# A two-layer hybrid DiT block: residual stores by unit from SP, squares in three tiles, weight loads at the start held back

## The chip, the cores and the metric

The kernel runs on one core of a Trainium2 chip. Its time is device microseconds of one execution, the median of several runs. The profile comes from one more execution. The engines are TensorE (PE, with its weight loads as PEld), VectorE (DVE), ScalarE (ACT), GpSimd (POOL) and SyncE (SP, which here only issues DMAs). Each engine works through its own queue strictly in order. A DMA is issued by an instruction in the queue of SP or POOL, which waits there until its data and its target are ready.

## The reference

Two layers of a transformer block on 512 tokens x (A) and 256 context tokens (C), with D = 1024 and a hidden width of 2816:

```python
for i in range(2):
    mx, mc = modulation(c, ada_w[i], ada_b[i]), modulation(c_ctx, ada_w[i], ada_b[i])
    x  = x  + 0.5*mx[2]*swiglu(pre_norm(x,  norm1_g[i], mx[0], mx[1]), ffn1...)
    xc = xc + 0.5*mc[2]*swiglu(pre_norm(xc, norm1_g[i], mc[0], mc[1]), ffn1...)
    ux, uc = pre_norm(x, norm2_g[i], mx[3], mx[4]) @ w_in[i], pre_norm(xc, ...) @ w_in[i]
    y, yc = four mixers (windowed attention, gated delta net, MLA, neighbourhood attention)
    x  = x  + mx[5] * (y @ w_out[i])
    x  = x  + 0.5*mx[8]*swiglu(pre_norm(x, norm3_g[i], mx[6], mx[7]), ffn2...)
    # the same for xc in layer 0 only
return rms_norm(x, final_norm_g)
# pre_norm(h, g, shift, scale) = rms_norm(h, g) * (1 + scale) + shift
# modulation(c, w, b) = silu(c) @ w + b, in nine parts
```

## The kernel before

The residual X lies in SBUF as `[128, 8, 768]`: eight chunks m (or k) of 128 features, 512 columns of A and 256 of C. A is cut into the units A0 and A1 of 256 columns; with C there are three units. Every product is made of three matmuls (`mm3`) of high and low halves, which is why each weight is loaded (`raw`, tile `wr`), cast on ACT (`wh`) and its rest formed on DVE (`wl`).

The stages are: start; first FFN of layer 0; mixers; `second_half` (output projection and second FFN); the same for layer 1. `ffn2` is the FFN of three of the four places (both layers' first FFN, and layer 0's second). It forms the hidden activations group by group and adds each group's down projection to X by an accumulating DMA from POOL (L509, from a tile `y`). For the last group it goes unit by unit, `PASSES[2]` = C, A0, A1, and for each unit through the eight chunks m (`down(..., True)`): 12 matmuls into `dacc`, then x is updated on DVE (L503), squared on ACT into a tile `sq` (L282) and the square added to the unit's sum `ss` on POOL (L283; on DVE for A1 from chunk 5). If the caller asks (`save`), chunk m of the unit is stored to DRAM from POOL's queue (L507, tensor `xd`); both first FFNs ask for it, for C and A in layer 0 and for A in layer 1, because `second_half` loads X back from there. Two chunks into the next unit (`LAG` = 2) `then(u)` is called for the unit before. It is `norm`: four `nsum` matmuls sum over partitions (L294), DVE and POOL form the reciprocal root (L308, L310), DVE a diagonal `dg` (L297), PE spreads it (`rb`, L301), and per chunk there are one ACT operation (L328) and two DVE operations (L324, L329) that write the next stage's input `xn`.

`sq` is one tile in these stages, shared by tag with an unused output of the adaLN reductions on DVE (`adao`, L211); in the last FFN (`ffn`) there are two.

The mixers start with projections `pj` from the weights `win` (loaded by SP, L350); the tiles of the mixers lie over X and the FFN's weight tiles, and wait for these tile by tile.

At the start SP loads X, then 32 tiles of adaLN weights `adaw` (L178, 256 KB each), which PE multiplies with silu(c) (L179). `ada_row` loads `silr` (L165, 1 MB, silu'd on ACT), which only the later adaLN reductions on DVE need. Then C, A0 and A1 are squared and normed, and the FFN's weights are asked for by `raw` in 256 KB loads, in eight tiles by turns.

The order in each engine's queue isn't the order of the code: a planner lays it down when the program is built, by simulating the engines and taking what it finds ready, earlier code first. So a stage's instructions may stand before or behind those of its neighbours.

Of the kernel before, what the change touches and what calls it, by code (L numbers as in the profile page):

```python
# [6 lines left out]
F32 = mybir.dt.float32  # L7
# [9 lines left out]
TX = 512  # L17
TC = 256
# [31 lines left out]
class Net:  # L50
# [111 lines left out]
    def ada_row(self):  # L162
        nc = self.nc
        self.silr = self.const.tile([128, 2, 1024], F32, name="silr")
        nc.sync.dma_start(out=self.silr, in_=self.I["crow"].rearrange("(o v) k -> o v k", o=1).to_broadcast([128, 2, 1024]))  # L165
        nc.scalar.activation(self.silr, self.silr, ACTF.Silu)

    def ada_first(self):

        nc = self.nc  # L170
        acc = self.psum(name="adaacc", ring="r")
        for k in range(KD):
            for g in range(4):
                if g >= 2:
                    w = self.wp.tile([128, 512], F32, tag="wr", name="adaw", bufs=RB)
                else:
                    w = self.hp.tile([128, 768], F32, tag=("hh", "hl")[g % 2], name="adaw")[:, :512]
                nc.sync.dma_start(out=w, in_=self.I["ada_w0"][k * 128:(k + 1) * 128, g * 512:(g + 1) * 512])  # L178
                nc.tensor.matmul(acc[32 * g:32 * g + 32, :], lhsT=self.silc[:, k], rhs=w,  # L179
                                 start=(k == 0), stop=(k == KD - 1), tile_position=(0, 32 * g))  # L180
        tp = self.ada_rows(acc)
        src = tp.rearrange("p s (g r) -> p g s r", r=32)[:, :, :, 0:2]
        self.ada_bias(0, 0, src, 4)
        self.mod_cols(0, 1, 2)
# [77 lines left out]
    def sumsq(self, u, m, eng=None):  # L262

        nc = self.nc
        p, c, t = self.unit(u)
        if self.wblk:
            if u == "A":
                for h in ("A0", "A1"):
                    self.sumsq(h, m, nc.vector)
                return  # L270
            if m == 0:
                self.ss[u] = self.wp.tile([128, 512], F32, tag="ws", name="ss" + u, bufs=4)[:, :t]
            ss = self.ss[u]
        else:
            if m == 0 and c.start == 0:
                self.ss[p] = self.fs.tile([128, self.T[p]], F32, tag="ss" + p, name="ss" + p, bufs=1)
            ss = self.ss[p][:, c]
        if m == 0:
            nc.scalar.activation(ss, self.X[p][:, m, c], ACTF.Square)
        else:  # L280
            sq = self.fs.tile([128, TX], F32, tag="sq", name="sq", bufs=1 if self.wblk else 2)[:, :t]
            nc.scalar.activation(sq, self.X[p][:, m, c], ACTF.Square)  # L282
            (eng or (nc.vector if u == "A" or (u in SSV and m >= SSM) else nc.gpsimd)).tensor_tensor(ss, ss, sq, op=ALU.add)  # L283

# [70 lines left out]

    def raw(self, ap):
        t = self.wp.tile([128, 512], F32, tag="wr", name="wr", bufs=RB)[:, :ap.shape[-1]]
        self.nc.sync.dma_start(out=t, in_=ap)
        return t

# [64 lines left out]
    def ffn2(self, l, i, save, then):  # L425
# [3 lines left out]
        nc = self.nc  # L429
# [48 lines left out]
        def down(f0, f1, m, us, last):  # L478
            nf = f1 - f0
            while (l, 3 * i + 2) not in self.adone:  # L480
                self.sided += 1
                next(self.side)
            ap = dn[l, fi, m, :, f0:f1].rearrange("p f c -> p (f c)")
            if not last:
                wh, wl = self.weight(ap, nf * 128)
            else:
                if m not in keep:
                    keep[m] = self.block(self.raw(ap), [keep[w][m // 3][:, m % 3] for w in "hl"])
                wh, wl = keep[m]
            for v in us:  # L490
                p, cols, t = self.unit(v)
                r = 0 if p == "A" else 1
                acc = self.psum((128, t), name="dacc", ring=None if last else "d")
                if not last and v == us[0]:
                    y = self.wp.tile([128, TX + TC], F32, tag="y", name="y", bufs=3)
                for f in range(f0, f1):
                    c = slice((f - f0) * 128, (f - f0) * 128 + 128)
                    self.mm3(self.two(acc, v), wh[:, c], wl[:, c], self.tok(H[f][0], v), self.tok(H[f][1], v), f == f0, f == f1 - 1)
                if not last:
                    nc.scalar.activation(y[:, 0:TX] if p == "A" else y[:, TX:], acc, ACTF.Copy, scale=gate[:, i, m, r:r + 1])  # L500
                    continue
                x = self.X[p][:, m, cols]
                nc.vector.scalar_tensor_tensor(out=x, in0=acc, scalar=gate[:, i, m, r:r + 1], in1=x,  # L503
                                               op0=ALU.mult, op1=ALU.add)
                self.sumsq(v, m)
                if p in save:
                    nc.gpsimd.dma_start(out=self.xd[p][:, m, cols], in_=x)  # L507
            if not last:
                nc.gpsimd.dma_start(out=self.X[""][:, m], in_=y, accum_op=ALU.add)  # L509

# [4 lines left out]
        for t, f, n in order:  # L515
            if n == 0:
                chunks[f] = self.chunk7(up[l, fi, f], hid, f)
            next(chunks[f], None)
            if n == SLOTS - 1 and f == GROUPS2[gi][1] - 1 and f < NF - 1:
                tasks += [(t + WAIT, *GROUPS2[gi], m) for m in range(KD)]  # L520
                gi += 1
            if tasks and tasks[0][0] <= t:
                down(*tasks.pop(0)[1:], ("C", "A"), False)
            fill(nc1, (t + 1) / SLOTS)
        for k in tasks:
            down(*k[1:], ("C", "A"), False)
        keep = {w: [self.tp7.tile([128, 3, 512], F32R, tag="t%s%d" % (w, n), name="wt" + w) for n in range(3)] for w in "hl"}
        due = []
        for us in PASSES[2]:
            for m in range(KD):  # L530
                if due and m >= LAG:
                    then(due.pop(0))
                down(*GROUPS2[-1], m, us, True)
            due += us
        for u in due:
            then(u)

    def sums7(self):

# [1313 lines left out]
```

## Time and profile before

| | |
|---|---|
| median of 3 runs | 3258.91 us (3252.43 to 3259.69) |
| the profiled execution itself | 3246.65 us |
| its span, first to last instruction | 3244.9 us |
| PE busy | 3026.7 us (93%) |
| DVE busy | 2027.8 us (62%) |
| ACT busy | 1362.1 us (42%) |
| POOL busy | 560.6 us (17%) |
| mean granted TensorE clock | 0.957 |

Busy time counts the stretches in which an engine has an instruction under way. The granted clock is a share of 2.4 GHz: 1.00 is that level, 0.50 is 1.2 GHz. In a timeline a row shows the start, the duration, the engine and line, the operation with output<-input, and in brackets how long the engine had stood idle and what ended that.

### The profile page before, as it was taken

The page shows a single profiled execution, that of the slowest core. Times are in us where ns is not written, and L with a number is a line of the kernel's source. Part 1 is how long each engine was busy: PE and PEld are TensorE (multiplying, and loading weights), DVE is VectorE, ACT ScalarE, POOL GpSimd, SP SyncE. Part 2 cuts the span into 40 slices and gives each one's busy share as a digit, 9 for nine tenths or more (in the row PEclk, how much of TensorE's full clock was granted, in tenths as well). Part 3 has the DMA queues.
Part 4 walks back from the last instruction along what each step waited for, and adds up shares of the span by engine and source line. Part 5 has one row for each costly group of instructions (what it writes and reads, how often), then busy time and mean ns, then how long its engine had stood idle before and what let it go on. Part 6 is the DMA issues. An engine that isn't in the chain of part 4 may idle for free.

```text
span 3244.9 us, 49733 instructions
## 1 busy us (share of the span) xinstructions
PE 3026.7 (93%) x18880; PEld 2730.5 (84%) x18880; DVE 2027.8 (62%) x3766; ACT 1362.1 (42%) x2655; POOL 560.6 (17%) x814
## 2 busy tenths in 40 slices
PE   6899999798999998899999899999897899999998
PEld 3799999786888887799999889999786788788887
DVE  4999855536855349896557986556647744353334
ACT  3344444345444333444444334444455353342223
POOL 2212100411233012211112221111311332000001
PEclk8999999899999898999999899999898999899999
DMA  5578644214543243665552485555223623323333
GB/s 203 155 205 211 154 110 96 96 58 124 154 96 88 84 136 114 179 188 130 118 122 80 127 241 137 123 114 117 69 78 114 159 62 75 127 87 98 96 98 104
DMA packets 181392, 399.45 MB, mean 123 GB/s; under 512 B 23745, under 2 KB 58049, under 8 KB 181025
## 3 DMA queue, kind: packets, MB, share of 16 engines
q1 hardware_dynamic: 128352, 240.80, 24.4%
q0 software_dynamic: 52800, 155.48, 20.6%
q8 instruction: 148, 2.42, 0.3%
q14 instruction: 92, 0.75, 0.1%
HBM read 302.21 MB, written 39.65 MB: 105 GB/s over the span
## 4 chain that ended last, share of the span: by engine, by line
PE 76%; DVE 10%; DMA 5%; issue 5%; ACT 2%; POOL 1%; SPq 0%; DVEq 0%; POOLq 0%; ACTq 0%
PE dacc L370 6%; PE dacc L372 6%; PE dacc L371 6%; PE pb L370 3%; PE pb L371 3%; PE pb L372 3%; PE o L1012 3%; PE pj L370 3%; PE pj L372 3%; PE pj L371 3%; PE pc L370 2%; PE pa L372 2%; PE pc L372 2%; PE pc L371 2%; PE pa L370 2%
## 5 line engine op out<-in xcount | busy, mean ns | idle before, releaser
L334 ACT CAST wh<-wr 128x512 fp32r<-128x512 f32 (+6 forms) x523 | 348.6, 669 | 657.1 <-PE dacc L371 150.1
L339 DVE TENSOR_TENSOR wl<-wr,wh 128x512 fp32r<-128x512 f32 (+6 forms) x523 | 393.1, 754 | 266.4 <-ACT wh L334 254.0
L371 PE MATMUL dacc<-hl,wh 128*128 128x512 f32 (+1 forms) x1080 | 369.0, 342 | 9.6 <-DVE hl L339 9.6
L370 PE MATMUL dacc<-hh,wh 128*128 128x512 f32 (+1 forms) x1080 | 368.5, 343 | 1.9 <-ACT hh L334 0.9
L372 PE MATMUL dacc<-hh,wl 128*128 128x512 f32 (+1 forms) x1080 | 367.7, 342 | 1.4 <-DVE wl L339 1.4
L211 DVE CUSTOM_DVE_ANT_0 adao<-adaw,silr,adab 128x1024 bf16<-128x1024 f32 x224 | 293.2, 1309 | 35.2 <-DMA adaw<-ada_t 34.8
L370 PE MATMUL pj<-xnh,wh 128*128 128x256 f32 (+2 forms) x768 | 249.8, 326 | 5.5 <-ACT wh L334 5.0
L509 POOL DMA_DIRECT2D x<-y x144 | 125.4, 871 | 741.3 <-ACT y L500 721.2
L372 PE MATMUL pj<-xnh,wl 128*128 128x256 f32 (+2 forms) x768 | 244.0, 321 | 9.1 <-DVE wl L339 9.0
L371 PE MATMUL pj<-xnl,wh 128*128 128x256 f32 (+2 forms) x768 | 246.2, 321 | 0.0
L339 DVE TENSOR_TENSOR wl<-ws,wh 128x512 fp32r<-128x512 f32 x228 | 163.4, 717 | 130.5 <-ACT wh L334 130.5
L334 ACT CAST wh<-ws 128x512 fp32r<-128x512 f32 x228 | 141.0, 620 | 230.9 <-PE dacc L371 116.9
L371 PEld LDWEIGHTS dacc<-hl,wh 128*128 128x128 f32 x1080 | 204.1, 189 | 32.1 <-DVE hl L339 10.6
L370 PEld LDWEIGHTS dacc<-hh,wh 128*128 128x128 f32 x1080 | 204.1, 189 | 26.9 <-ACT y L500 2.7
L372 PEld LDWEIGHTS dacc<-hh,wl 128*128 128x128 f32 x1080 | 203.7, 189 | 26.6 <-DVE wl L339 1.6
L500 ACT ACTIVATE y<-dacc,modG 128x256 f32<-128x256 f32 (+1 forms) x288 | 166.1, 579 | 67.6 <-PE dacc L372 26.7
L372 PEld LDWEIGHTS pj<-xnh,wl 128*128 128x128 f32 (+1 forms) x768 | 148.6, 195 | 21.7 <-DVE wl L339 11.5
L370 PEld LDWEIGHTS pj<-xnh,wh 128*128 128x128 f32 (+1 forms) x768 | 150.3, 196 | 19.0 <-ACT wh L334 7.8
L370 PE MATMUL pa<-xnh,wh 128*128 128x384 f32 x456 | 155.4, 341 | 4.3 <-ACT wh L334 3.4
L372 PE MATMUL pa<-xnh,wl 128*128 128x384 f32 x456 | 154.4, 340 | 5.1 <-DVE wl L339 5.1
L371 PEld LDWEIGHTS pj<-xnl,wh 128*128 128x128 f32 (+1 forms) x768 | 150.5, 196 | 9.3 <-issue 1.1
L198 POOL DMA_DIRECT2D adaw<-ada_t x128 | 71.8, 561 | 500.3 <-DVE mod L211 416.8
(404 smaller groups left out, 8074.3 us busy)
## 6 DMA issues: line engine op xcount, KB each, us to landing
wr<-wgu SPq DMA_DIRECT2D x264, 256.0 KB, 3.6
adaw<-ada_t POOLq DMA_DIRECT2D x128, 512.0 KB, 4.3
x<-y POOLq DMA_DIRECT2D x144, 384.0 KB, 5.0
wr<-wd SPq DMA_DIRECT2D x144, 192.0 KB, 2.7
wr<-win SPq DMA_DIRECT2D x44, 512.0 KB, 3.7
wr<-wgu SPq DMA_DIRECT2D x44, 512.0 KB, 3.7
adaw<-ada_w SPq DMA_DIRECT2D x32, 256.0 KB, 5.4
wr<-wd SPq DMA_DIRECT2D x24, 320.0 KB, 2.9
```

The source lines that it names most:

```text
L198: nc.gpsimd.dma_start(out=w, in_=self.I["ada_t"][todo[n][0], todo[n][1]])
L211: nc.vector.tensor_tensor_reduce(o, ws[n], self.silr[:, v], 1.0, self.adab[:, l, m:m + 1], ALU.mult, ALU.add, self.mods[l][:, m, v:v + 1])
L334: nc.scalar.copy(hi, src)
L339: (nc.vector if leng == "V" else nc.gpsimd).tensor_tensor(lo, src, hi.bitcast(F32), op=ALU.subtract)
L370: nc.tensor.matmul(out, lhsT=wh, rhs=xh, start=start, stop=False, skip_group_check=more)
L371: nc.tensor.matmul(out, lhsT=wh, rhs=xl, start=False, stop=False, skip_group_check=more)
L372: nc.tensor.matmul(out, lhsT=wl, rhs=xh, start=False, stop=stop, skip_group_check=more)
L500: nc.scalar.activation(y[:, 0:TX] if p == "A" else y[:, TX:], acc, ACTF.Copy, scale=gate[:, i, m, r:r + 1])
L509: nc.gpsimd.dma_start(out=self.X[""][:, m], in_=y, accum_op=ALU.add)
L1012: nc.tensor.matmul(o[:, q0 + q], lhsT=p[:, q * 128:q * 128 + 128], rhs=v(kb), start=False, stop=kb == 3 and q == n // 128 - 1)
```

## The change

Three edits. (1) In `ffn2`, the stores of X to `xd` go from one per chunk (128 KB) in POOL's queue to one per unit (1 MB) in SP's queue; they are issued by a new function `close`, just before `then(u)`. (2) In the stages that use `ffn2` the square goes to a tile of the tag `y`, of which there are three in turn, and not to the single `sq`. (3) At the start, the load of `silr` and the first four loads through `raw` each get a one-column copy on POOL ahead of them, which reads the last adaLN weight tile and writes the load's target; so they are issued only when that tile has landed and the copy is done.

```diff
     def ada_row(self):
         self.silr = self.const.tile([128, 2, 1024], F32, name="silr")
+        nc.gpsimd.tensor_copy(self.silr[:, 0, 0:1], self.late)
         nc.sync.dma_start(out=self.silr, in_=self.I["crow"]...)
...
     # ada_first, behind the loop over the 32 tiles
+        self.late = w[:, 0:1]
+        self.gated = 4
...
     # sumsq
-            sq = self.fs.tile([128, TX], F32, tag="sq", name="sq", bufs=1 if self.wblk else 2)[:, :t]
+            if self.wblk:
+                sq = self.wp.tile([128, TX + TC], F32, tag="y", name="sq", bufs=3)[:, :t]
+            else:
+                sq = self.fs.tile([128, TX], F32, tag="sq", name="sq")[:, :t]
...
     def raw(self, ap):
         t = self.wp.tile([128, 512], F32, tag="wr", name="wr", bufs=RB)[:, :ap.shape[-1]]
+        if self.gated:
+            self.gated -= 1
+            self.nc.gpsimd.tensor_copy(t[:, 0:1], self.late)
         self.nc.sync.dma_start(out=t, in_=ap)
...
     # ffn2, down(), last group
                 self.sumsq(v, m)
-                if p in save:
-                    nc.gpsimd.dma_start(out=self.xd[p][:, m, cols], in_=x)
...
+        def close(u):
+            p, cols, _ = self.unit(u)
+            if p in save:
+                nc.sync.dma_start(out=self.xd[p][:, :, cols], in_=self.X[p][:, :, cols])
+            then(u)
+
         due = []
         for us in PASSES[2]:
             for m in range(KD):
                 if due and m >= LAG:
-                    then(due.pop(0))
+                    close(due.pop(0))
                 down(*GROUPS2[-1], m, us, True)
             due += us
         for u in due:
-            then(u)
+            close(u)
```

## Rows read from the trace of the kernel before

**Rows 1.** The page, busy time of the matmul engine and the others.

```profile
PE 3026.7 (93%) x18880; PEld 2730.5 (84%) x18880; DVE 2027.8 (62%) x3766; ACT 1362.1 (42%) x2655; POOL 560.6 (17%) x814
```

**Rows 2.** Windows: length, busy PE, PEld, DVE, ACT, POOL, clock, DMA share, GB/s.

```profile
580.00:595.60 15.60, 15.55 (x130) 15.34 (x128) 5.08 (x12) 1.56 (x4) 8.24 (x14) 1.00 0.27 94
595.60:622.10 26.50, 6.09 (x19) 4.34 (x19) 18.20 (x42) 14.21 (x32) 12.71 (x22) 0.55 0.22 71
2325.40:2346.10 20.70, 5.33 (x18) 3.87 (x17) 14.96 (x35) 11.29 (x25) 7.82 (x14) 0.58 0.05 14
1777.00:1791.60 14.60, 7.88 (x26) 5.60 (x25) 14.60 (x32) 4.46 (x11) 3.70 (x4) 0.58 0.10 36
```

**Rows 3.** Timeline of PE at the ends of both layers' first FFN.

```profile
595.27 0.28 PE L372 MATMUL dacc<-hh,wtl 128*128 128x256 f32 x1
...
618.35 1.01 PE L294 MATMUL nsum<-ones,ssA 128*128 128x1 f32 x4 [5.00 <-DVE ssA L283]
...
622.09 0.78 PE L370 MATMUL pj<-xnh,wh 128*96 128x256 f32 x1
...
2325.16 0.28 PE L372 MATMUL dacc<-hh,wtl 128*128 128x256 f32 x1
...
2339.81 0.99 PE L294 MATMUL nsum<-ones,ssA 128*128 128x1 f32 x4 [5.10 <-DVE ssA L283]
...
2343.46 0.78 PE L370 MATMUL pj<-xnh,wh 128*96 128x256 f32 x1
```

**Rows 4.** Timeline of SP before layer 1's mixers.

```profile
2286.30 0.81 SPq L350 DMA_DIRECT2D wr<-win  x2
```

**Rows 5.** Timeline of POOL in the last down projection of layer 0's first FFN.

```profile
569.32 1.76 POOL L507 DMA_DIRECT2D xdC<-x  x3 [30.53 <-DVE x L503]
571.09 0.75 POOL L283 TENSOR_TENSOR ssC<-ssC,sq 128x256 f32<-128x256 f32 x1
571.77 2.69 POOL L507 DMA_DIRECT2D xdC<-x  x5
...
598.23 0.72 POOL L283 TENSOR_TENSOR ssC<-ssC,sq 128x256 f32<-128x256 f32 x1 [0.53 <-ACT sq L282]
```

**Rows 6.** Line L507: duration min/median/max in ns, first and last start; landing.

```profile
L507 POOL DMA_DIRECT2D xdA<-x x32: 539/543/605, 575.2 to 2326.6; - x32
...
DMA to landing us min/median/max: 2.0/2.1/3.5
```

**Rows 7.** Timeline of PE at the end of layer 0's second FFN.

```profile
1776.62 0.47 PE L372 MATMUL dacc<-hh,wtl 128*128 128x256 f32 x1
...
1782.83 1.01 PE L294 MATMUL nsum<-ones,ssA 128*128 128x1 f32 x4 [1.13 <-DVE ssA L283]
```

**Rows 8.** Timelines of POOL and DVE there.

```profile
1757.68 0.74 POOL L283 TENSOR_TENSOR ssC<-ssC,sq 128x256 f32<-128x256 f32 x1 [0.53 <-ACT sq L282]
...
1778.61 0.47 DVE L503 SCALAR_TENSOR_TENSOR x<-dacc,modG,x 128x256 f32<-128x256 f32 x1
```

**Rows 9.** DMA issues: operation, count, KB each, median us to landing.

```profile
wr<-win SPq DMA_DIRECT2D x44, 512.0 KB, 3.7
...
x<-xT SPq DMA_DIRECT2D x2, 1024.0 KB, 6.8
```

**Rows 10.** Timeline of PE at the start, second half of the adaLN stream.

```profile
30.20 11.20 PE L179 MATMUL adaacc<-adaw,silc 128*32 128x512 f32 x32 [2.15 <-DMA adaw<-ada_w]
```

**Rows 11.** Line L197, the one-column copies on POOL: ns min/median/max.

```profile
L197 POOL COPY adaw<-xnl x2: 174/942/1711, 78.6 to 80.2; 128x1 f32<-128x1 f32 x2
```

**Rows 12.** Timeline of DVE at the start.

```profile
40.59 0.43 DVE L283 TENSOR_TENSOR ssA<-ssA,sq 128x256 f32<-128x256 f32 x1 [0.48 <-ACT sq L282]
...
44.03 1.28 DVE L339 TENSOR_TENSOR wl<-wr,wh 128x512 fp32r<-128x512 f32 x2
```

**Rows 13.** Timeline of ACT at the start.

```profile
30.29 1.89 ACT L166 ACTIVATE silr<-silr 128x2048 f32<-128x2048 f32 x1
...
41.92 2.70 ACT L334 CAST wh<-wr 128x512 fp32r<-128x512 f32 x5
```

## The prediction

> **What bounds the kernel now.** I read the page's busy shares first: TensorE is busy 93% of the span [rows 1], so time can be won only where PE stands still. The row of tenths shows where that is: the first slice, and a dip after each FFN. I then cut windows around the dips. With 15.55 us busy of 15.6 and the clock at 1.00, PE never waits inside the last down projection of layer 0. In the 26.5 us behind it PE shows 6.09 us, with the clock at 0.55. Behind the same place in layer 1 lies a stretch like it, 20.7 us long with 5.33 busy [rows 2].
>
> In order of time, PE's last down matmul of layer 0 ends at 595.27 + 0.28 = 595.55, and the next projection starts at 622.09: a hole of 26.5 us. In layer 1 it is 2325.44 to 2343.46, 18.0 us [rows 3]. Both times the projection comes 3.7 us behind the `nsum` of A1 (618.35 to 622.09, 2339.81 to 2343.46). In layer 1 its weight had been asked for at 2286.30, long before [rows 4]. So the hole ends when A1's sum of squares is there, not when a load is.
>
> Why is that sum late? POOL's own timeline says it. A store `xdC<-x` stands ahead of the first add, five stand between the first add and the second, and the seventh add of C runs at 598.23, after PE has finished all three units [rows 5]. A store holds POOL for only 0.54 us [rows 6], but POOL works in order, and each store waits for its own chunk's x, which PE delivers every 12 x 0.12 = 1.44 us (130 matmuls in 15.55 us, 12 to a chunk and unit [rows 2]). An add behind four stores of later chunks therefore waits about four chunks. The norms of C, A0 and A1, which should run under the next unit's matmuls, run one after another behind the last.
>
> The same function also runs as second FFN of layer 0, where it stores nothing: a control inside the profile. There the add of C's seventh square is done by 1757.68 + 0.74, some 19 us before the last down matmul, which ends at 1776.62 + 0.47 = 1777.09, and A1's `nsum` starts at 1782.83, 5.7 us behind it [rows 7, 8]. In layer 0's first FFN the same distance is 618.35 - 595.55 = 22.8 us.
>
> **Stores by unit from SP.** Removed from POOL: 40 issues (24 in layer 0, 16 in layer 1) of 0.543 us, 21.7 us of busy time [rows 6], worth nothing by itself; what counts is that the adds lose what they queue behind. Added to SP: five issues of 1 MB, at some 0.4 us each, as for `win` [rows 4]. C's and A0's stores leave under the next unit's matmuls, while SP has nothing else to fetch (the last group's weights are kept), so they cost nothing; without that cover they would cost their landing, 6.8 us for 1 MB [rows 9].
>
> A1's store is the one in the open. On SP, ahead of the next stage's weights, it waits for A1's last x. In the control, where norms share the DVE with these updates, the last x is done at 1778.61 + 0.47, 2.0 us behind the last matmul [rows 8]. So `win` is issued at about 2.0 + 0.4 + 0.4 + 0.1 = 2.9 us, lands 3.7 us later by its median, and up to 2.15 to 3.1 us later still if the store goes first: 2.15 is what 1 MB of `silr` cost the adaLN loads [rows 10], 3.1 is 6.8 - 3.7, 1 MB against 512 KB [rows 9]. With 2.15 the load is there at 8.8, and a cast of about 1 us makes 9.8. By the sums the projection starts at 5.7 + 3.7 = 9.4. The two paths end close together; I take 10 us for each hole. Lower bound 5.6: x, square and add with no DVE backlog (0.47, 0.53 with hand-overs [rows 8], 0.43 for an add on DVE [rows 12], and as much again on the way to `nsum`: 1.9) and 3.7. Upper bound: the store moves at the pace of the old ones, 8 x 2.1 = 16.8 us [rows 6], `win` lands 2.9 + 16.8 + 3.7 = 23.4 behind the matmuls, and the hole is 24.5 with the cast.
>
> The Trainium skill, DMA: Bandwidth & Descriptors, section Queues, rings and completion order, says that each DMA engine consumes the descriptors of one ring in ring order; by that rule the store, now in the same SP ring as `win`, is served wholly before it, where from POOL's queue the two would have interleaved. No row of this profile has a store and a load in that order; with the rule the hole is 9.8, without it 9.4 by the sums.
>
> So layer 0 gives 26.5 - 10 = 16.5 us and layer 1 18.0 - 10 = 8.0, together 24.5. The stretch at half speed stays: the clock reads 0.58 in the control's short hole too [rows 2]. The tiles that the mixers lay over X must now wait for A1's store, issued by 2.4 us and, at 6.8, landed by 9.2. That is hidden by A1's norm, which reads the same X, starts only behind `nsum` at 5.7 and has 16 DVE operations of some 0.47 us, 7.5 in all; without that cover it would cost some 3.5 us.
>
> **Squares in three tiles.** With one tile, square and add alternate, 0.53 + 0.74 = 1.27 us an add [rows 8]. That is under PE's 1.44 per chunk, so in the passes it costs nothing and frees nothing but perhaps 1 us for A1; at the start it keeps the squares (whose last add ends at 40.59 + 0.43 = 41.02 [rows 12], beside the adaLN stream's end) from becoming the bound there. The tiles are those of `y`, whose last use lay over 30 us before the first square (POOL idle 30.53 [rows 5]).
>
> **Later loads at the start.** PE waits 2.15 us in the middle of the adaLN stream, where `silr` was loaded, and ends it at 41.40 [rows 10]. With `silr` behind the stream it ends at about 39.25: 2.15 gained. Five one-column POOL copies join, 0.17 to 1.71 us each in the only two that exist [rows 11]; with POOL else idle I take the low one. Against it, the first four weight loads now follow the stream and `silr`. Today five casts run from 41.92 [rows 13], and the DVE's halves (1.28 for two [rows 12]) while it waits for C's norm. Moved to about 46 (39.25 + 0.4 + 3.7 + 2.15, and a hand-over), four halves (2.6 us) fall inside C's norm, where the DVE is busy, as `silr`'s Silu (1.89 us [rows 13]) falls on ACT. Bounds: -3 us (all hidden, and `mod` no longer behind a half) to 2.6 + 1.9 - 2.15 = +2.4. I take half of the halves: -1 us.
>
> **Sum.** -16.5 - 8.0 - 1.0 = -25.5. The profiled execution itself took 3246.65 us (span 3244.9), which makes 3221; it lies 12 us under the median of the runs shown, 3258.91, and 6 under the lowest. Set against that median: 3233 us.
>
> **Rivals.**
> (a) The forecast: both holes shrink to about 10 us. 3233; its own range 3225 to 3241.
> (b) More: the backlog is smaller than the control's, where POOL and adaLN work also pressed on the DVE; holes of 7 and a start of -3: 19.5 + 11 + 3 = 33.5, so 3225. For it: three squares; against it: the load's path.
> (c) Part: the wait moves to SP. `win` behind a store that is ordered late, or adds that queue behind something else; holes of 16: 10.5 + 2 = 12.5, so 3246. For it: in layer 1 `win` was early and now cannot be.
> (d) No change: the order on POOL isn't set by the stores but by late squares, and the sums come as late as now; 3255 to 3260. The control speaks against it.
> (e) Slower: A1's store crawls at the rate of eight old ones in series. Holes of 24.5 in both layers, and a start of +2.4: -2.0 + 6.5 + 2.4 = +6.9, so 3266. It decides once the store takes over some 13 us: from there the holes average over 21. Against it: 1 MB of x lands in 6.8 us [rows 9].
>
> **How the numbers follow.** What a measurement of this kernel can tell from no change is about 0.2%, 6.5 us. Chances: (a) 0.50, (b) 0.20, (c) 0.17, (d) 0.08, (e) 0.05. Faster by over 0.2% are (a), (b) and (c): 0.87; within 0.2% (d): 0.08; slower (e): 0.05. The range takes in (b) and (c) with some 5 us of spread of the runs (3252.43 to 3259.69) on either side: 3219 to 3250.
>
> **What would show it.** On POOL, C's seven adds follow C's matmuls at 0.75 to 1.44 us apart, and C's `nsum` stands among A0's matmuls. Both holes are 8 to 12 us, with A1's `nsum` 4 to 6 us behind the last down matmul. SP shows five 1 MB stores, A1's within 3 us of that matmul, landing in 5 to 9 us. The adaLN stream runs without a gap and ends near 39. The forecast fails if C's `nsum` still comes after the last matmul (d), if `win` lands over 15 us behind it (c, e), or if the first FFN matmul starts over 3 us later than now.

## The result, and the profile after

The changed kernel took 3214.52 us (median of 4 runs, 3206.72 to 3224.58) against 3259.3 us before: a ratio of 0.9867, 95% interval [0.9831, 0.9902]. Measured a second time beside other experiments it was 0.9898 [0.9867, 0.9929]. One of the second measurement's six runs took 9953.84 us at a granted clock of 0.423 and is left out of every figure here. The medians of the runs of both measurements are 3219.6 us for the changed kernel (9 runs) and 3257.0 us for the one before (59 runs, those beside the changed kernel's second measurement and beside the experiments): some 37 us, or 1.15%. The forecast was 25.5 us. It is faster, as forecast, and by more: the first measurement lies 4.5 us under the range, the second, with a median of 3220.6 us, inside it.

The two profiled executions differ by only 27 us, 3246.65 to 3219.6. Where that comes from is at the end of this part; first the stages. The page's row of busy times of the changed kernel:

```profile
PE 3030.6 (94%) x18880; PEld 2737.9 (85%) x18880; DVE 2023.0 (63%) x3766; ACT 1361.0 (42%) x2655; POOL 544.6 (17%) x779
```

PE does the same work [rows 1]; what changed is where it stands still. The timeline of PE at the two holes of [rows 3]:

```profile
597.81 0.28 PE L382 MATMUL dacc<-hh,wtl 128*128 128x256 f32 x1
600.54 1.01 PE L301 MATMUL nsum<-ones,ssA 128*128 128x1 f32 x4 [2.45 <-DVE ssA L290]
603.21 1.19 PE L308 MATMUL rb<-dg,ones 128*128 128x256 f32 x2 [1.66 <-DVE dg L304]
608.40 0.53 PE L380 MATMUL pj<-xnh,wh 128*96 128x256 f32 x1 [4.00 <-ACT wh L341]
...
2310.41 0.28 PE L382 MATMUL dacc<-hh,wtl 128*128 128x256 f32 x1
2313.14 0.70 PE L301 MATMUL nsum<-ones,ssA 128*128 128x1 f32 x4 [2.46 <-DVE ssA L290]
2315.81 1.19 PE L308 MATMUL rb<-dg,ones 128*128 128x256 f32 x2 [1.98 <-DVE dg L304]
2320.32 0.53 PE L380 MATMUL pj<-xnh,wh 128*96 128x256 f32 x1 [3.31 <-ACT wh L341]
```

From 598.09 to 608.40 and from 2310.69 to 2320.32: holes of 10.3 and 9.6 us, where 10 had been forecast for each. `nsum` is no longer what `pj` waits for: it comes 2.45 us behind the last matmul, and the last 4.0 us are the wait for the cast of `win`. POOL shows why the sum is early. All seven adds of C run in one group, under the passes, with no store between them as in [rows 5]:

```profile
570.73 5.66 POOL L290 TENSOR_TENSOR ssC<-ssC,sq 128x256 f32<-128x256 f32 x7 [31.10 <-ACT sq L289]
```

On SP, layer 0's A1 store is issued 0.8 us behind the last matmul, and `win` behind it (the second line takes four loads together; the first is issued at its start):

```profile
598.92 0.53 SPq L539 DMA_DIRECT2D xdA<-x  x1
...
600.50 11.77 SPq L357 DMA_DIRECT2D wr<-win  x4
```

The surplus is elsewhere. These are the windows of three stages that follow each other, in before: output projection and norms, layer 0's second FFN, layer 1's first FFN (columns as in [rows 2]):

```profile
1138.60:1227.20 88.60, 74.14 (x449) 66.16 (x449) 46.47 (x98) 30.54 (x69) 10.91 (x14) 0.92 0.43 130
1227.20:1777.10 549.90, 530.61 (x3098) 499.84 (x3098) 410.33 (x714) 240.63 (x464) 90.95 (x113) 0.97 0.53 135
1777.10:2325.45 548.35, 530.32 (x3096) 500.33 (x3096) 376.34 (x656) 234.62 (x452) 93.14 (x121) 0.97 0.52 135
```

and in the changed kernel:

```profile
1137.30:1234.60 97.30, 74.36 (x448) 66.07 (x448) 81.74 (x155) 29.73 (x69) 22.42 (x28) 0.88 0.62 194
1234.60:1787.70 553.10, 532.46 (x3099) 499.57 (x3099) 432.61 (x762) 241.50 (x467) 104.06 (x137) 0.97 0.59 157
1787.70:2310.70 523.00, 520.71 (x3103) 495.90 (x3101) 322.81 (x563) 239.51 (x462) 70.75 (x76) 0.99 0.43 100
```

Layer 1's first FFN is 25 us shorter: PE idles 2.3 us in it and not 18.0, the DVE has 93 instructions less, and the DMAs move 100 GB/s and not 135. The two stages ahead of it are 8.7 and 3.2 us longer, with more DVE instructions. The source view of the line of the adaLN reductions says what has moved. Before:

```profile
L211 DVE CUSTOM_DVE_ANT_0 adao<-adaw,silr,adab x224: 1265/1277/2876, 85.4 to 1958.2; 128x1024 bf16<-128x1024 f32 x112
```

and in the changed kernel, with the first and last start in us:

```profile
L215 DVE CUSTOM_DVE_ANT_0 adao<-adaw,silr,adab x224: 1264/1277/2866, 84.2 to 1549.9; 128x1024 bf16<-128x1024 f32 x112
```

The same 224 reductions, but the last starts at 1549.9 and not at 1958.2. In before, 48 of them ran between 1777 and 1960, in layer 1's first FFN; they kept the DVE busy for 63.2 us. In the changed kernel they run in layer 0's second FFN, and of the 80 ahead of them 32 run in the output projection and norms, where 4 did. Their unused output `adao` had shared its single tile with `sq`. So a reduction could not be placed ahead of squares that stand earlier in the code, and the squares at the end of layer 0's second FFN stand ahead of these 48. Once `sq` has its own tiles, the planner issues the reductions as soon as it finds room.

The start: the adaLN stream has no gap and ends at 39.30, as forecast, but the first FFN matmul comes at 56.26, 0.9 us later than before.

```profile
17.38 21.92 PE L180 MATMUL adaacc<-adaw,silc 128*32 128x512 f32 x64 [17.38 <-ACT sq L289]
...
56.26 0.58 PE L380 MATMUL gu<-xnh,wh 128*128 128x256 f32 x1 [0.98 <-ACT xnh L335]
```

The place of the missing gain, 27 us and not 37, in the profiled executions can be named too: layer 0's mixers (from `pj` at 608.40 to the first `wo` at 1137.31) took 528.9 us and before 516.5. In a second profile of the changed kernel they took 517.3, and its span is 3204.0. Nearly all of the 11.6 us between these two lies in one stretch at the clock's lower level, shown below: up to it the two profiles, counted from `pj`, are 0.3 us apart. The changed kernel met the long form of it in the first profile and the short form in the second.

### The profile page after: what moved, and what is told of

Its sections match the earlier page's. It is cut to its first block, busy times and chain, and to the rows that moved or that the text cites. A ratio compares the mean times of both kernels' runs of the same rounds, so it can differ in the third digit from the quotient of the medians.

```text
span 3217.8 us, 49777 instructions
## 1 busy us (share of the span) xinstructions
PE 3030.6 (94%) x18880; PEld 2737.9 (85%) x18880; DVE 2023.0 (63%) x3766; ACT 1361.0 (42%) x2655; POOL 544.6 (17%) x779
## 3 DMA queue, kind: packets, MB, share of 16 engines
q1 hardware_dynamic: 133552, 246.04, 25.4%
## 4 chain that ended last, share of the span: by engine, by line
PE 78%; DVE 9%; DMA 5%; issue 4%; ACT 2%; POOL 1%; SPq 0%; DVEq 0%; POOLq 0%; ACTq 0%
PE dacc L380 6%; PE dacc L382 6%; PE dacc L381 6%; PE o L1026 3%; PE pb L380 3%; PE pb L381 3%; PE pb L382 3%; PE pj L380 2%; PE pj L382 2%; PE pj L381 2%; PE pc L380 2%; PE pc L382 2%; PE pc L381 2%; PE pa L382 2%; PE pa L380 2%
## 5 line engine op out<-in xcount | busy, mean ns | idle before, releaser
L380 PE MATMUL pj<-xnh,wh 128*128 128x256 f32 (+2 forms) x768 | 248.7, 325 | 12.2 <-ACT wh L341 11.6
L382 PE MATMUL pb<-th,wl 128*128 128x384 f32 x456 | 154.3, 338 | 2.4 <-DVE wl L346 2.4
```

The costliest lines, as they stand in the source:

```text
L380: nc.tensor.matmul(out, lhsT=wh, rhs=xh, start=start, stop=False, skip_group_check=more)
L382: nc.tensor.matmul(out, lhsT=wl, rhs=xh, start=False, stop=stop, skip_group_check=more)
```

## The experiments

Each ratio is to before, with its 95% interval. "Holes" are those behind the last down projection of layer 0's and layer 1's first FFN, as above. "Three stages" is the time from the first `wo` matmul of layer 0 to the end of layer 1's first FFN, read off PE's timeline, as the sum of the windows above (1186.8 before, 1173.4 in the changed kernel).

| kernel | ratio | holes, us | three stages, us | last reduction starts, us |
|---|---|---|---|---|
| before | 1 | 26.5, 18.0 | 1186.8 | 1958 |
| all edits | 0.9867 [0.9831, 0.9902] | 10.3, 9.6 | 1173.4 | 1550 |
| all edits, again | 0.9898 [0.9867, 0.9929] | 10.2, 9.1 | 1173.6 | 1534 |
| stores only | 0.9944 [0.9925, 0.9963] | 10.8, 10.1 | 1182.6 | 1962 |
| squares only | 0.9942 [0.9922, 0.9962] | 21.3, 9.4 | 1173.0 | 1545 |
| one square tile, untied | 0.9980 [0.9959, 1.0001] | 26.5, 18.0 | 1177.8 | 1546 |
| start only | 1.0000 [0.9982, 1.0018] | 26.5, 18.0 | 1183.9 | 1956 |
| squares only, last batch held | 0.9956 [0.9939, 0.9973] | 21.3, 9.4 | 1186.3 | 1988 |
| all edits, last batch held | 0.9894 [0.9864, 0.9923] | 11.3, 9.2 | 1180.3 | 1987 |
| all edits, second batch held | 0.9825 [0.9797, 0.9853] | 10.2, 8.5 | 1155.4 | 1645 |
| all edits, no late store | 0.9900 [0.9877, 0.9924] | 7.8, 6.3 | 1173.0 | 1548 |
| all edits, stores from POOL | 0.9896 [0.9870, 0.9922] | 9.3, 9.3 | 1170.2 | 1541 |
| second batch held, A1's store halved | 0.9829 [0.9795, 0.9863] | 8.5, 7.3 | 1153.5 | 1646 |

**Stores only.** The first edit alone.

```diff
-                if p in save:
-                    nc.gpsimd.dma_start(out=self.xd[p][:, m, cols], in_=x)
...
+            if p in save:
+                nc.sync.dma_start(out=self.xd[p][:, :, cols], in_=self.X[p][:, :, cols])
+            then(u)
```

> Only the stores are changed: by unit from SP; one square tile as before, start as before. Theory 1 (stores and adaLN reductions are two separate gains): the holes behind both first FFNs shrink from 26.5 and 18.0 us to 9 to 11, the last adaLN reduction still runs at about 1935 to 1960 us, and the whole is some 24 us (0.7%) faster than before. Theory 2 (the squares' single tile is what makes the sums late, the stores hardly matter): the holes stay above 15 us and the whole gains less than 10 us. Theory 3 (one gain that needs both edits): less than 10 us here and less than 10 us with the squares alone.

Holes of 10.8 and 10.1 us, last reduction at 1962: theory 1 in its mechanism. PE in layer 0, whose last down matmul ends at 598.70:

```profile
603.05 1.01 PE L294 MATMUL nsum<-ones,ssA 128*128 128x1 f32 x4 [4.35 <-DVE ssA L283]
...
609.47 0.53 PE L370 MATMUL pj<-xnh,wh 128*96 128x256 f32 x1 [2.11 <-ACT wh L334]
```

The gain is 0.56%, 18 us, and not 24.

**Squares only.** The second edit alone.

```diff
+            if self.wblk:
+                sq = self.wp.tile([128, TX + TC], F32, tag="y", name="sq", bufs=3)[:, :t]
```

> Only the squares are changed: three tiles of tag y in turn. Theory 1: what counts is that the squares no longer share a tile with the unused output of the adaLN reductions; 48 reductions move from layer 1's first FFN (1775 to 1958 us) into layer 0's second, the last runs near 1550, the holes behind the first FFNs stay at about 26 and 18 us, and the whole is 15 to 25 us faster. Theory 2: the sums come earlier, the holes shrink to 10 us, and the gain comes from there. Theory 3 (my prediction's own term): within 3 us of before.

As fast as the stores alone, and the reductions have moved, as theory 1 says. But its holes were expected to stay; layer 0's shrank to 21.3 us and layer 1's to 9.4. POOL's timeline in layer 1:

```profile
2285.39 4.83 POOL L286 TENSOR_TENSOR ssC<-ssC,sq 128x256 f32<-128x256 f32 x6 [30.79 <-ACT sq L285]
2290.36 0.61 POOL L510 DMA_DIRECT2D xdA<-x  x1
2290.98 0.76 POOL L286 TENSOR_TENSOR ssC<-ssC,sq 128x256 f32<-128x256 f32 x1
2291.73 0.58 POOL L510 DMA_DIRECT2D xdA<-x  x1
2292.33 0.75 POOL L286 TENSOR_TENSOR ssA<-ssA,sq 128x256 f32<-128x256 f32 x1
```

Squares that needn't wait for the add before them let six adds of C run without a pause, 4.83 us in all, so that they are done before A0's stores begin; after that an add stands behind a store or two. Where C isn't stored, that is enough. In layer 0, where C's own stores stand ahead of its adds, the hole is still 21.3. So in layer 1 the late sums of the kernel before needed both, stores in POOL's queue and a square that waits for its tile: each edit alone removes the better part of that hole, and there the two gains don't add.

**One square tile, but untied.** The square keeps one tile, of another tag (that of the FFN's silu output).

```diff
-            sq = self.fs.tile([128, TX], F32, tag="sq", name="sq", bufs=1 if self.wblk else 2)[:, :t]
+                sq = self.fs.tile([128, 384], F32, tag="sg", name="sq", bufs=1)[:, :t]
```

> As before, but the square has one single tile of a tag that it doesn't share with the adaLN reductions (it shares with the silu output sg of the FFN). Theory 1 (the shared tile holds the reductions back): as with three square tiles, 15 to 25 us faster, last reduction near 1550 us. Theory 2 (the number of square tiles counts): as before, within 3 us.

```profile
L211 DVE CUSTOM_DVE_ANT_0 adao<-adaw,silr,adab x224: 1266/1277/2866, 84.2 to 1546.1; 128x1024 bf16<-128x1024 f32 x112
```

This tells the two properties of the second edit apart. The reductions move with one tile as with three (last start 1546), and layer 1's first FFN falls to 523.4 us. So it is the shared tile that had held them, not the number of tiles. The holes stay at 26.5 and 18.0: for these one tile is not enough. In all the gain is 0.2%, 6.5 us, with an interval that reaches no change, where I expected 15 to 25 us. Its output projection and norms are 99.3 us long, 10.8 more than before; 36 reductions run on the DVE there, and 4 in the kernel before.

**Start only.** The third edit alone.

```diff
+        nc.gpsimd.tensor_copy(self.silr[:, 0, 0:1], self.late)
...
+            self.nc.gpsimd.tensor_copy(t[:, 0:1], self.late)
```

> Only the start is changed: silr and the first four FFN weight loads behind the adaLN stream. By my prediction: 1 us faster (bounds -3 to +2.4). By the profile of the changed kernel: stream without a gap, first FFN matmul about 1 us later than before, clock back 2 us earlier, in all between -1 and +1 us; nothing that the times can tell from no change.

No change, as the profile said; the first FFN matmul starts at 55.83, 0.4 us later.

**All edits, the last batch held.** Against the changed kernel:

```diff
-            if js[0][0] == 0 and js[0][1] < 8 and n < AB:
+            if (js[0][0] == 1 or js[0][1] < 8) and n < AB:
```

> The changed kernel, but the last batch of adaLN reductions (48, code of layer 1's first FFN) is held there by a one-column copy ahead of its first loads, the way the first batch already is. Theory 1 (the changed kernel's surplus over my forecast comes from these 48 reductions having left layer 1's first FFN for layer 0's second): 8 to 15 us slower than the changed kernel, at a ratio of about 0.991 to before; the last reduction runs near 1940 us, PE loses some 20 us more from 1764 to 2030 and some 10 us less from 1450 to 1530. Theory 2 (the three square tiles by themselves give the surplus): as the changed kernel, within 3 us.

The windows of the same three stages:

```profile
1146.30:1244.10 97.80, 74.64 (x448) 66.14 (x448) 81.92 (x155) 29.74 (x69) 22.92 (x28) 0.88 0.61 193
1244.10:1784.70 540.60, 526.98 (x3099) 498.50 (x3099) 380.64 (x662) 242.63 (x467) 82.06 (x97) 0.97 0.49 122
1784.70:2326.60 541.90, 528.25 (x3102) 498.09 (x3101) 376.70 (x663) 236.92 (x462) 95.02 (x118) 0.99 0.52 135
```

With the 48 reductions back in layer 1's first FFN, this stage loses 18.9 us of the 25.4 and layer 0's second FFN gets 12.5 back: 6.9 us against the changed kernel. By the times it is 0.27% against the first measurement of the changed kernel and nothing against the second; the intervals overlap. (The profiled run, 3242.0 us, is the slowest of its six.) So the stages speak for theory 1, a little under its 8 to 15 us, and the times alone don't decide.

**Squares only, the last batch held.** The same gate on the kernel with the second edit alone.

> Only the squares are changed (three tiles), and the last batch of 48 reductions is held in layer 1's first FFN as in the experiment before. By the stage sums of the two earlier runs (with three tiles alone 95.5 + 555.6 + 522.0 us from the output projection to the end of layer 1's first FFN; with all edits and the held batch 97.8 + 540.6 + 541.9): 1180, that is 7 us more than three tiles alone, and about 0.996 to before. If the reductions' move were the whole gain of the three tiles: no faster than before (0.999 to 1.001).

The three stages take 1186.3 us, 13.3 more than with the squares alone, twice what I expected, and no less than before. Taking the rows of the table together: where the last batch stays in its place (before, stores only, start only, and the two with it held) the three stages are 1180 to 1187, mean 1184; where it moves, with three square tiles (all edits twice, squares only, no late store, stores from POOL), 1170.2 to 1173.6. In these stages the move of the reductions is worth some 11 us (6.9 by the one pair of kernels, 13.3 by the other), and three tiles by themselves nothing. The ratio, 0.9956, is below the 0.999 to 1.001 of the other case, since the holes are still 21.3 and 9.4: these 13.8 us are 0.42%. By the times, 0.9942 against 0.9956, the move is worth 5 us, and the intervals overlap: it is the stages that show it, the times don't.

**All edits, the second batch held.** The code of the second batch (80 reductions) stands behind the norms ahead of layer 0's second FFN. In the changed kernel 32 of them run before and among these norms (the 155 DVE instructions of the window above, against 98 before).

```diff
-            if js[0][0] == 0 and js[0][1] < 8 and n < AB:
+            if js[0][0] == 0 and n < AB:
```

> The changed kernel, but the second batch of adaLN reductions (80) is held by the same one-column copy until the norms ahead of layer 0's second FFN are done. Theory: in the changed kernel some 40 of them stand ahead of or among these norms on DVE and PE waits 7.8 us twice where it waited 5.7 before; here these two waits go back to at most 6 us in all, the first gu there starts 7 to 9 us earlier against the stage before, and the whole is about 7 us (0.2%) faster than the changed kernel. Rival: the reductions are only pushed to the stretch around 1550 us and cost the same there: within 2 us of the changed kernel.

```profile
1138.20:1217.40 79.20, 71.29 (x448) 64.01 (x448) 41.91 (x90) 30.08 (x69) 8.70 (x12) 0.97 0.42 131
1217.40:1769.90 552.50, 532.36 (x3099) 500.33 (x3099) 468.81 (x827) 240.78 (x467) 117.60 (x157) 0.98 0.63 174
1769.90:2293.60 523.70, 521.01 (x3102) 495.82 (x3101) 322.92 (x563) 239.44 (x462) 71.34 (x76) 0.99 0.42 100
```

Output projection and norms take 79.2 us, against 97.3 in the changed kernel and 88.6 before: the DVE has 90 instructions there, and no reduction. Layer 0's second FFN takes the reductions in with 552.5 us, as long as in the changed kernel with 65 DVE instructions less, so the rival falls. The gain is 18 us in the stages, where I expected 7. With 3204.36 us and 0.9825 it is faster than before, and by its median than both measurements of the changed kernel; its interval lies below the second's and overlaps the first's.

**All edits, no store behind the last pass.** A1's columns are stored before their pass, so the stored A1 lacks the last group's down projection.

```diff
+            if p in save and u != "A1":
...
+            if u == "C" and "A" in save:
+                nc.sync.dma_start(out=self.xd["A"][:, :, TC:TX], in_=self.X["A"][:, :, TC:TX])
```

> The changed kernel, but A1's columns are stored ahead of their pass, so that what is stored for A1 leaves out the last group's down projection; no store is left behind the last down projection. Theory (win waits behind the store in SP's ring; it landed 6.8 us after its issue, where its median is 3.7): win lands 3.7 us after its issue, the holes behind the first FFNs shrink from 10.3 to about 7.2 us in layer 0 and from 9.6 to about 6.5 in layer 1, some 6 us (0.2%) in all. Rival (the store doesn't delay win): holes of 9.5 to 10.3 us as now.

Holes of 7.8 and 6.3 us: the size was right. SP and ACT of this kernel in layer 0, the issue of `win` and the cast that waits for its landing:

```profile
598.70 1.17 SPq L357 DMA_DIRECT2D wr<-win  x2
...
604.18 1.04 ACT L341 CAST wh<-wr 128x1024 fp32r<-128x1024 f32 x1 [2.14 <-DMA wr<-win]
```

`win` lands 5.5 us after its issue, not 3.7. In the changed kernel, where its cast starts at 607.30, it was 6.8. So between these two profiles the landing differs by 1.3 us. The other half is the issue, 1.2 us earlier against the last matmul (598.70 - 597.46 against 600.50 - 598.09). Together 2.5, which is 10.3 - 7.8. That `win` still takes more than 3.7 may come from two loads of the mixers' constants, 448 and 64 KB, issued 1.3 and 0.9 us ahead of it in the same queue; no run takes these away.

In layer 1 the 3.3 us come another way:

```profile
2301.83 15.37 SPq L357 DMA_DIRECT2D wr<-win  x3
...
2312.00 0.61 PE L301 MATMUL nsum<-ones,ssA 128*128 128x1 f32 x4 [2.46 <-DVE ssA L290]
...
2315.85 0.50 PE L380 MATMUL pj<-xnh,wh 128*96 128x256 f32 x1
```

With no A1 store to stand behind in SP's queue, `win` is issued 7.7 us before the last matmul's end (2309.55) and not 2.0 behind it, as in the changed kernel (2312.64 against 2310.68), and the hole ends with the sums, 3.85 us behind `nsum`. There A1's store costs because SP takes its queue in order and waits for A1's last x. The time doesn't show the 5.8 us of both layers: 0.9900, no better than the changed kernel.

**All edits, the unit's store from POOL.**

```diff
-                nc.sync.dma_start(out=self.xd[p][:, :, cols], in_=self.X[p][:, :, cols])
+                nc.gpsimd.dma_start(out=self.xd[p][:, :, cols], in_=self.X[p][:, :, cols])
```

> The changed kernel, with its stores by unit, but issued from POOL's queue instead of SP's. Theory 1 (what counted was that few stores by unit stand where no add queues behind them; the queue matters by 1 to 3 us at most): holes of 8 to 11 us, whole within 4 us of the changed kernel. Rival (it was leaving POOL's queue that counted): adds of the next unit queue behind the store, and holes of 15 us and more. By the ring order, win is then no longer behind the store and lands 3.7 to 5 us after its issue instead of 6.8.

```profile
601.40 0.88 POOL L539 DMA_DIRECT2D xdA<-x  x1 [0.30 <-DVE xnl L336]
...
608.49 1.04 ACT L341 CAST wh<-wr 128x1024 fp32r<-128x1024 f32 x1 [0.38 <-DMA wr<-win]
```

Holes of 9.3 us: it was few stores at the unit's end that counted, not leaving POOL. But in layer 0 `win`, issued at 601.52 on SP, 0.12 us behind the store on POOL, is cast 7.0 us later, not the 3.7 to 5 that I expected by the order of rings. In layer 1 `win` is issued at 2262.53, 40 us before the last matmul's end, so the 9.3 us there have nothing to do with its landing: `pj` waits for its cast, which stands behind six of the norm's operations in ACT's queue.

**All edits, once more.** No edit.

> The changed kernel once more, with more rounds, beside the two below. Expected: ratio 0.985 to 0.990 to before. In the profiled execution: holes of about 10 us, last reduction near 1550 us. Open: whether the 41 us at the lower clock level near 1070 us (17 us in the profile of before) come back. If they belong to the change, layer 0's mixers take some 12 us more than in before again; if they are chance, the stretch is 17 us in some executions, and the time that the profile of the changed kernel showed was 12 us unlucky.

Ratio 0.9898, holes 10.2 and 9.1, and layer 0's mixers in 517.3 us: the stretch is 17 us this time, so the long form does not belong to this kernel as such.

**Second batch held, A1's store in two halves.**

```diff
+                ks = slice(KD // 2 if u == "A1" else 0, KD)
+                nc.sync.dma_start(out=self.xd[p][:, ks, cols], in_=self.X[p][:, ks, cols])
...
+                if us == ["A1"] and m == KD // 2 - 1 and "A" in save:
+                    nc.sync.dma_start(out=self.xd["A"][:, 0:KD // 2, TC:TX], in_=self.X["A"][:, 0:KD // 2, TC:TX])
```

> The changed kernel with the second batch of reductions held behind the norms, and A1's store cut in two: chunks 0 to 3 are stored when they are done, only 512 KB are left behind the last down projection. Theory (the store ahead of win delays its landing, the amount by its size): holes of some 8.5 us instead of 10.2 and of some 7.5 to 8 instead of 9.6, 3 us less in all than with the second batch held alone; ratio 0.980 to 0.984 to before. Rival (size doesn't matter, only that a store is ahead): holes as now.

Holes of 8.5 and 7.3, about as expected; in layer 0 `win` lands 5.5 us after its issue (599.88 to 605.39), as with no store at all. The 2.8 us are too few for the times to tell: 3201.8 us, 0.9829, the same as with the store whole.

## Why the prediction was right, and where it fell short

**The holes.** Right in size, and in mechanism with one cause left out. 16.5 and 8.0 us were forecast; the profiled executions show 26.5 - 10.3 = 16.2 and 18.0 - 9.6 = 8.4, and the stores alone 15.8 and 7.9. The load's path set the end, as the 9.8 against 9.4 had it, though with other parts: the sums' path is shorter than forecast (`nsum` 2.45 us behind the last matmul, not 5.7; 4.35 with the stores alone, so three squares give 1.9 of it where I allowed 1), and the load lands later (6.8 us after its issue, where 3.7 + 2.15 = 5.85 was the sum). That stores queued ahead of the adds was not the only cause. The stores alone suffice for nearly all of both holes; but three square tiles, with the stores still in POOL's queue, also took 5.2 of layer 0's 26.5 and 8.6 of layer 1's 18.0. And in layer 1 the load's path is one that the change itself made: `win` had been asked for early, and now stands behind A1's store.

By the Trainium skill, DMA: Bandwidth & Descriptors, section Queues, rings and completion order, each DMA engine consumes descriptors in ring order, but a later one may finish its write before an earlier one. "Served wholly before it" went further than that rule. No run here shows that this order sets the price: in layer 0 `win` landed 6.8 us after its issue behind a store in the same queue, and 7.0 us behind one in the other queue.

**The squares.** This is the step that failed: "it costs nothing and frees nothing but perhaps 1 us for A1". I costed the chain of square and add, and named the other user of the tile, `adao`, only in the description of the kernel. I didn't ask which instructions had been kept in their place by it. So the gain of letting them go stood in the sum at nothing. The term is some 11 us in the three stages, which the untied square and the two held batches show: layer 1's first FFN 25 us shorter, the stages ahead of it 12 us longer (13.5 us in the two profiled executions). With it the forecast of 3233 becomes 3222, 7 us above the first measurement and 1 above the second, which is within the spread of the runs. That these 11 us carried the time under the range is read from the stages; the times of whole kernels don't show them, since with the last batch held the ratio is 0.9894, between the two without. "Costs nothing" also failed within the passes: with the stores in POOL's queue the three tiles shorten the holes by 13.8 us; only beside the first edit is their share down to 0.5 us a hole. Rival (b), more gain, comes nearest by its number, 3225, but by luck: its reason was a smaller backlog, which does show in the sums but not in the holes.

**The start.** 1 us of gain was forecast; it is none (1.0000), and 0.9 us later at the first FFN matmul in the profile. The stream ends where forecast; five of the later weights' halves, 0.7 us each on the DVE, and the Silu of `silr` on ACT fall into C's norm, where I took half of the halves.

**The base.** The profiled execution that the rows come from had a granted clock of 0.957, near the top of what 59 runs of before show (0.948 to 0.959, mean 0.953). The forecast was rightly set against the median of the runs instead. But the change also moves the mean clock: the 9 runs of the changed kernel have 0.955 to 0.963. "The stretch at half speed stays" was too strong: behind layer 0's hole, the first 10 us of the projections now have a clock of 0.77 (609.00 to 619.00), and had 0.68 (622.70 to 632.70).

**The sum.** 16.2 + 8.4 of holes and 11 for the reductions, less 0.9 at the start, are 35 us; measured are 37 from the medians. That they come so close is in part luck: the mixers are left out, and those of both layers together took 9.4 us more than before in the one profile of the changed kernel and 2.3 less in the other. The product of the three single ratios, 0.9944 x 0.9942 x 1.0000 = 0.9886, also lies between the two measurements, but layer 1's hole is in both factors, so that agreement isn't a proof. The single edits gained less in the times than their parts give: the stores 18 us where their holes give 23.7, the squares 19 where holes and stages give 27.6. In the profile of the squares the rest is in the mixers, 10.8 us longer in both layers together; that of the stores, the longest of its 12 runs, has layer 0's mixers at 538.9 us, in part through the stretch below. Why the mixers are longer isn't settled.

Of the rivals (c) and (e), a wait that moves to SP, (c)'s ground came true in layer 1: `win` had been early and now cannot be. Taking the store away shows what it costs, 2.5 and 3.3 us of hole. In the changed kernel it lands 7.2 and 5.4 us after its issue, against the 13 us from which (e) would have decided. (d) fell with the holes.

## What to carry to other kernels

A tile that two unrelated streams share is an order between them, even where one of the two writes only what nobody reads; before costing an edit that changes a tile's tag or number, list everything else that is allocated from it and see what would move. Work that is set free so may move as early as the planner finds room, not where it is useful: here it crowded the norms, and a one-column copy that holds it back until these are done was worth more (18 us) than its release (11 us). In an engine's in-order queue a store costs its wait for data and not its issue; put it where nothing queues behind it, and in a shape that needs few waits.

## What the runs showed of the hardware

**One stretch at the lower clock, in two lengths.** In layer 0's mixers the clock falls to its lower level behind gaps of 2.5 and 2.8 us on PE (1068.47 to 1071.02 and 1076.48 to 1079.28 in the changed kernel) and stays there for a long or a short time: by the mean clocks below some 41 us in the first profile of the changed kernel, (1 - 0.66) x 60 / 0.5, and 17 in the second, behind gaps of the same length. The window of either takes in the second gap and what follows:

```profile
1060.00:1120.00 60.00, 53.69 (x289) 46.06 (x283) 20.93 (x53) 17.50 (x34) 4.99 (x7) 0.66 0.27 85
```

```profile
1056.00:1116.00 60.00, 53.61 (x371) 46.38 (x369) 21.77 (x56) 22.51 (x42) 4.99 (x7) 0.86 0.27 85
```

PE is as busy in both, 53.7 and 53.6 us, but at 0.66 and 0.86, and does 289 and 371 matmuls. The mixers take 528.9 and 517.3 us: 11.6 us of difference between two executions of one kernel. Why the one execution had the long form and the other the short one, no run shows. Of the 13 profiles six have the long form, all of kernels that store by unit from SP, and of these only the second profile of the changed kernel has the short one. Whether that edit makes the long form likelier, and so gives back a part of its gain, stays open.

**What a store costs a load.** In layer 0 a 512 KB load (`win`) behind a 1 MB store of the same queue landed 6.6 to 7.8 us after its issue in five profiles (6.8 in the changed kernel, 7.8 with the last batch held). Behind a 1 MB store of another queue it was 7.0, with no store 5.5, and with 512 KB of store ahead 5.5, each in one profile. So 1 MB cost it 1.1 to 2.3 us; I had allowed 2.15 to 3.1. In layer 1 it was 5.5 to 6.6 us behind 1 MB and 4.6 behind 512 KB; without the store `win` is issued before the matmuls end there, so no figure is to be set beside these.
